# Weight parts in tiles of 1024 columns, one split for several products of a block of seven, and variances issued first

## The chip, the cores and the metric

The kernel runs on one core of one Trainium2 chip. The metric is the device time of one execution in microseconds (us). Three runs of the kernel before the change give a median of 1121.44 us (1121.39 to 1121.47).

## The reference

A two-layer transformer in float32 over 512 tokens of width 1024, with 256 memory tokens. Layer 0 mixes tokens by a gated chunk mixing (gMLP) and attends to the memory; layer 1 mixes by causal attention with forget gates ("fox") and attends to the memory. Each layer ends in a gated feed-forward of hidden width 2816.

```python
for layer in range(DEPTH):
    a = rmsnorm(h, ln_mix_pre[layer])
    mem_n = rmsnorm(mem, ln_mem[layer])
    ...   # main: spatial gating (layer 0) or forgetting attention (layer 1)
    mixed = jnp.concatenate([main, memory_attention(q_mem, mem_n, w_mem_kv[layer])], axis=-1)
    h = h + rmsnorm(mixed @ w_out[layer], ln_mix_post[layer])
    f = rmsnorm(h, ln_ffn_pre[layer])
    f = (jax.nn.silu(f @ w_ffn_gate[layer]) * (f @ w_ffn_up[layer])) @ w_ffn_down[layer]
    h = h + rmsnorm(f, ln_ffn_post[layer])
```

## The kernel before, in words

**Split products.** TensorE (PE) multiplies fp32r numbers. To keep the accuracy, each operand is split in two parts: `split` (L240-241) casts the value to fp32r on ScalarE (ACT), which is `whi`, and VectorE (DVE) subtracts that from the value, which is `wlo`. `mm3` (L191-195) then issues three matmuls per product: high by high (L193), high weights by low inputs (L194), low weights by high inputs (L195). So the first two of three need only `whi`, the third needs `wlo`.

**Weights.** SyncE (SP) loads 128x1024 fp32 values (512 KB) into one of four `raw` tiles. Their parts go to rings of eight tiles of 128x512 for `whi` and eight for `wlo` (`pair_of_parts`). A part is used by the PE until its tile comes free for a later part; a cast that finds no free tile waits for the PE, and everything behind it on ACT waits too, since each engine takes its instructions in the order in which they were issued.

**Blocks of seven.** Gate and up weights of the feed-forward are multiplied by Strassen's scheme in Winograd's form (class `Seven`): 8 half-width products become seven of 12 matmuls of 128x256, 84 in all, for 1024x256 weights. A block loads two raw tiles, w1 = (a11, a12) and w2 = (a21, a22). `sums` (L966) forms on DVE s3 = a11+a21 (L970), then rewrites the raw values in place: a21 (L972), a11 (L974), a12 (L975). Product 1 takes a11 before and product 2 a12 before they are rewritten; products 6 and 3 take a11 and a12 after, 5 and 4 take a21 and a22, 7 takes s3. Outputs are the PSUM tiles `a` (products 1, 6, 5), `e` (7, 4) and `x` (2, 3). ACT copies an output out after products 1 (L988), 5 (L997), 6 (L1000) and 7 (L1003); `end` (L1005) adds on DVE: L1008 (e), L1009 (a), L1011 (x), and then the rows of the gate or up side (L1063-1071). Two blocks, one for gate and one for up, make a pair. The order of products in a block is 1, 7, 2, 6, 4, 3, 5; in the first pair of each layer, whose inputs are ready one after the other, it is 1, 2, 3 of both blocks, then 7 and 6 of both, then 4 and 5 of both (`sevens`, L1017). Each layer has 10 pairs in four groups, with the down products of a group (L1117-1126) between.

**Norms.** `Norm.finish` (L281) has the PE sum squares into `st`, DVE adds epsilon (`var`, L292), GpSimd (POOL) raises to the power -1/2 (`r`, L262), and the PE broadcasts the result by transposes (`rb`, L259). The memory's norm in layer 0, and two halves at each boundary before a feed-forward or before layer 1's queries, go this way.

**What sets the order.** A scheduler of the tile framework places each instruction on its engine by its own estimate of when it is ready and by program order as priority; the source does not fix it. In layer 0's last pair, the normed memory of layer 1 (`mparts`, 8 activations and 8 DVE operations) is made between the last two blocks.

## Time and profile before

| | |
|---|---|
| median of 3 runs | 1121.44 us |
| profiled execution | 1121.42 us |
| its span, granted PE clock | 1119.7 us, 0.999 |
| PE busy | 1107.3 us (99%) |
| DVE busy | 892.0 us (80%) |
| ACT busy | 660.3 us (59%) |
| POOL busy | 28.5 us (3%) |
| HBM read | 104.71 MB |
| casts `whi` <- raw, 128x512 | 460, 276.2 us, mean 620 ns |
| subtractions `wlo`, 128x512 | 460, 305.2 us, mean 685 ns |

The span runs from the first to the last recorded instruction; 1.7 us of the profiled time lie outside it. Rows of the timeline give the start and the duration in us, the engine, the source line, the operation, output and inputs by name, the shape and the number of instructions of a run, and in brackets how long the engine was idle before and what released it. Matmuls overlap: a 128x256 matmul is recorded with 0.28 us, and the next starts 0.12 us after it.

The program's places in the trace of before: layer 0's mixing from 0 to 165 us, the boundary to 210, its feed-forward to 527, layer 1's queries to 595, fox attention to 760, a boundary to 798, layer 1's feed-forward from there.

### The profile page before, as it was taken

What the parts mean: (1) busy time and instruction counts of PE and PEld (TensorE: products, weight loads), DVE (VectorE), ACT (ScalarE), POOL (GpSimd) and SP (SyncE); (2) the same over time, 40 slices, a digit from 0 to 9 for tenths busy, and PEclk for the clock granted to TensorE, in tenths of its full rate; (3) what the DMA queues carried; (4) which work ended last, traced back from release to release, by engine and by line L of the source; (5) the groups of instructions that cost most, each with busy time, mean ns of one, the idle gap of its engine ahead of it and who ended that gap; (6) DMA issues with size and microseconds to landing.
All of it is one profiled execution on the core that took longest, in us unless ns stands there. A gap on an engine that the chain in (4) does not pass through costs nothing.

```text
span 1119.7 us, 19536 instructions
## 1 busy us (share of the span) xinstructions
PE 1107.3 (99%) x7409; PEld 1002.7 (90%) x7409; DVE 892.0 (80%) x1721; ACT 660.3 (59%) x1388; POOL 28.5 (3%) x41
## 2 busy tenths in 40 slices
PE   8999999999999999999999999999999999999998
PEld 6998889999899899998988898889999899899996
DVE  7979448999598578796968889958998598588776
ACT  7775458755266255476757677768765266255453
POOL 0100001000000000001000000001000000000000
PEclk9999999999999999999999999999999999999999
DMA  7413231334224234244242655421235234233222
GB/s 265 151 49 109 77 97 58 100 108 151 76 89 140 74 99 127 76 135 148 63 128 59 153 128 137 135 76 57 65 106 152 74 101 133 70 109 118 76 76 76
DMA packets 63557, 118.12 MB, mean 105 GB/s; under 512 B 5164, under 2 KB 39992, under 8 KB 63464
## 3 DMA queue, kind: packets, MB, share of 16 engines
q1 hardware_dynamic: 62584, 116.05, 33.8%
q8 instruction: 58, 0.95, 0.4%
q0 software_dynamic: 192, 0.52, 0.2%
q10 hardware_dynamic: 688, 0.31, 0.1%
q14 instruction: 35, 0.29, 0.1%
HBM read 104.71 MB, written 2.10 MB: 95 GB/s over the span
## 4 chain that ended last, share of the span: by engine, by line
PE 86%; DVE 7%; ACT 3%; issue 2%; POOL 1%; DMA 1%; SPq 0%; POOLq 0%; DVEq 0%; ACTq 0%
PE y L193 9%; PE y L195 9%; PE y L194 9%; PE a L194 5%; PE a L193 5%; PE a L195 5%; PE ps L195 3%; PE ps L194 3%; PE ps L193 3%; PE e L193 3%; PE e L194 3%; PE x L194 3%; PE x L193 3%; PE x L195 3%; PE e L195 3%; DVE wlo L241 2%
## 5 line engine op out<-in xcount | busy, mean ns | idle before, releaser
L241 ACT CAST whi<-raw 128x512 fp32r<-128x512 f32 x460 | 276.2, 620 | 267.0 <-PE y L195 118.6
L241 DVE TENSOR_TENSOR wlo<-raw,whi 128x512 fp32r<-128x512 f32 x460 | 305.2, 685 | 108.8 <-ACT whi L241 106.6
L193 PE MATMUL y<-whi,fhi 128*128 128x512 f32 (+1 forms) x356 | 140.0, 394 | 0.0
L194 PE MATMUL y<-wlo,fhi 128*128 128x512 f32 (+1 forms) x356 | 139.4, 392 | 0.0
L195 PE MATMUL y<-whi,flo 128*128 128x512 f32 (+1 forms) x356 | 139.4, 392 | 0.0
L194 PE MATMUL a<-xslo,whi 128*128 128x256 f32 x320 | 90.0, 281 | 0.0
L194 PE MATMUL x<-xslo,whi 128*128 128x256 f32 x320 | 89.9, 281 | 0.0
L195 PE MATMUL x<-xshi,wlo 128*128 128x256 f32 x320 | 89.9, 281 | 0.0
L193 PE MATMUL x<-xshi,whi 128*128 128x256 f32 x320 | 89.8, 281 | 0.0
L193 PE MATMUL a<-xshi,whi 128*128 128x256 f32 x320 | 89.8, 281 | 0.0
L195 PE MATMUL a<-xshi,wlo 128*128 128x256 f32 x320 | 89.8, 281 | 0.0
L193 PEld LDWEIGHTS y<-whi,fhi 128*128 128x128 f32 x356 | 66.9, 188 | 15.7 <-ACT fhi L241 0.7
L195 PEld LDWEIGHTS y<-whi,flo 128*128 128x128 f32 x356 | 66.9, 188 | 15.5 <-DVE flo L241 0.2
L194 PEld LDWEIGHTS y<-wlo,fhi 128*128 128x128 f32 x356 | 67.0, 188 | 14.7 <-DVE wlo L241 0.2
L193 PE MATMUL ps<-xshi,whi 128*128 128x256 f32 (+1 forms) x224 | 67.5, 304 | 0.0
L195 PE MATMUL ps<-xshi,wlo 128*128 128x256 f32 (+1 forms) x224 | 67.1, 302 | 0.1
L194 PE MATMUL ps<-xslo,whi 128*128 128x256 f32 (+1 forms) x224 | 66.4, 299 | 0.0
L193 PEld LDWEIGHTS a<-xshi,whi 128*128 128x128 f32 x320 | 60.4, 189 | 0.4
L194 PEld LDWEIGHTS a<-xslo,whi 128*128 128x128 f32 x320 | 60.3, 188 | 0.3
L193 PEld LDWEIGHTS x<-xshi,whi 128*128 128x128 f32 x320 | 60.4, 189 | 0.0
L195 PEld LDWEIGHTS x<-xshi,wlo 128*128 128x128 f32 x320 | 60.3, 189 | 0.0
L194 PEld LDWEIGHTS x<-xslo,whi 128*128 128x128 f32 x320 | 60.3, 188 | 0.0
(283 smaller groups left out, 3091.1 us busy)
## 6 DMA issues: line engine op xcount, KB each, us to landing
raw<-in_w_gate SPq DMA_DIRECT2D x44, 512.0 KB, 3.6
raw<-in_w_up SPq DMA_DIRECT2D x44, 512.0 KB, 3.5
raw<-in_w_down SPq DMA_DIRECT2D x44, 512.0 KB, 4.0
raw<-in_w_out SPq DMA_DIRECT2D x16, 512.0 KB, 4.5
raw<-in_w_b_q SPq DMA_DIRECT2D x8, 512.0 KB, 3.5
raw<-in_w_a_v SPq DMA_DIRECT2D x6, 512.0 KB, 7.0
raw<-in_w_a_u SPq DMA_DIRECT2D x6, 512.0 KB
raw<-in_w_v SPq DMA_DIRECT2D x6, 512.0 KB, 3.7
```

The source lines that it names most:

```text
L193: PE.matmul(o, w[0], x[0], start=start, stop=False, skip_group_check=more)
L194: PE.matmul(o, w[0], x[1], start=False, stop=False, skip_group_check=more)
L195: return PE.matmul(o, w[1], x[0], start=False, stop=stop, skip_group_check=more)
L241: last_parts[:] = A.copy(hi, src), (eng or V).tensor_sub(lo, src, hi)
```

## The change

It does three things.

1. The rings of parts hold four tiles of 128x1024 in place of eight of 128x512, of the same bytes. `prepared` weights still are split in steps of 512 columns, but into the two halves of one tile, which comes free when the whole tile has been used.
2. Where 1024 columns are split for products that lie close together, one cast and one subtraction do it: in a block of seven for products 1 and 2, for 6 and 3, for 5 and 4 (product 7 stays alone with 512 columns, in a tile of 1024), in the down products between groups, and in the gate weights `w_a_u` of layer 0. On ACT and on DVE each, 316 instructions of 512 columns become 158: 126 of 128x1024 and 32 of 128x4x2x128. DVE goes from 1721 to 1563 instructions.
3. `var` and `rsqrt` of `Norm.finish` are issued with high priority.

PE, POOL and SP have the same number of instructions as before; what the scheduler does with the new sizes moves some of them. `var` of the memory's norm in layer 0 stands right behind the first `q` product on DVE, ahead of 5 `mparts` and 8 subtractions, where it had 4 of these subtractions and the `mparts` before it, and its `rb` stands 12 matmuls earlier on the PE. At the boundaries the first half's `var` and its `rb` stand earlier too, `rb` by 11 matmuls. The order is the same in both layers at the first two of the following places.

**Place 1: ACT, first pair of a feed-forward (layer 0).** `raw_2506` holds w1 of the first block, `raw_2569` w1 of the second; `a_2511` is the output of product 1 of the first block. Before:

```order
L1095 COPY y_2436<-y_2486 128x512
L1095 COPY y_2437<-y_2494 128x512
L241 CAST whi_2553<-raw_2506 128x512
L988 COPY s_1_2513<-a_2511 128x256
L241 CAST whi_2580<-raw_2569 128x512
```

Now, with `raw_2432` and `raw_2491` for the two w1, `a_2437` for that output, `whi_2475` for products 6 and 3 of the first block and `whi_2502` for 1 and 2 of the second:

```order
L1108 COPY y_2362<-y_2412 128x512
L1108 COPY y_2363<-y_2420 128x512
L1001 COPY s_1_2439<-a_2437 128x256
L246 CAST whi_2475<-raw_2432 128x1024
L246 CAST whi_2502<-raw_2491 128x1024
L246 CAST whi_2534<-raw_2491 128x1024
L1001 COPY s_2_2498<-a_2496 128x256
```

The cast for product 3 stood ahead of the copy of product 1's output and now stands behind it, with twice the columns. On the PE the rows that follow product 2 (`whi_2443` in tile 1) now are:

```order
L200 MATMUL x_2436<-xshi_1960,wlo_2444 128x256
L198 MATMUL x_2436<-xshi_2103,whi_2475 128x256
L199 MATMUL x_2436<-xslo_2104,whi_2475 128x256
L198 MATMUL a_2437<-d2hi_2327,whi_2475 128x256
L199 MATMUL a_2437<-d2lo_2328,whi_2475 128x256
L198 MATMUL a_2496<-xshi_1874,whi_2502 128x256
L199 MATMUL a_2496<-xslo_1875,whi_2502 128x256
L198 MATMUL x_2495<-xshi_1923,whi_2502 128x256
L200 MATMUL x_2436<-xshi_2103,wlo_2476 128x256
```

Where the 12 matmuls of product 3 followed in a piece, two of product 3, two of product 6, two of product 1 of the second block and one of its product 2 now come before the first that reads a low part.

**Place 2: ACT, the third block (first of the second pair).** Before, `whi_2850` (product 6), `whi_2867` (4), `whi_2883` (3) and `whi_2899` (5) are the parts of the third block:

```order
L241 CAST whi_2850<-raw_2786 128x512
L241 CAST whi_2867<-raw_2788 128x512
L241 CAST whi_2883<-raw_2786 128x512
L997 COPY s_1_2513<-a_2511 128x256
L241 CAST whi_2899<-raw_2788 128x512
L1064 ACTIVATE s_1_2514<-s_1_2514 128x512
L997 COPY s_2_2576<-a_2574 128x256
L1064 ACTIVATE s_1_2513<-s_1_2513 128x512
L241 CAST whi_2934<-raw_2923 128x512
L988 COPY s_3_2793<-a_2791 128x256
```

Now these are `whi_2748` (6 and 3) and `whi_2765` (5 and 4):

```order
L1010 COPY s_1_2439<-a_2437 128x256
L1077 ACTIVATE s_1_2440<-s_1_2440 128x512
L1010 COPY s_2_2498<-a_2496 128x256
L1077 ACTIVATE s_1_2439<-s_1_2439 128x512
L1001 COPY s_3_2695<-a_2693 128x256
L246 CAST fhi_2430<-s_2_2499 128x512
L1016 COPY s_3_2696<-e_2694 128x256
L246 CAST fhi_2428<-s_2_2498 128x512
L246 CAST whi_2748<-raw_2688 128x1024
L246 CAST whi_2765<-raw_2690 128x1024
```

The casts stood ahead of the closing of the first pair (the activations L1064) and now stand behind it, and behind the copies of the third block's own products 1 (`a_2693`) and 7 (`e_2694`, L1016). On the PE, product 7 is followed by the 12 matmuls of product 2, then two of 6, two of 3 and two of 4, and then those that read low parts.

**Place 3: DVE, the last block of layer 0 (the twentieth).** Before, `wlo_5823` is for product 7, `wlo_5852` for 6:

```order
L246 SCALAR_TENSOR_TENSOR mparts_5643<-mem_5617,gains,mparts_5643 128x256
L1008 TENSOR_TENSOR s_19_5658<-e_5656,s_19_5658 128x256
L975 TENSOR_TENSOR raw_5787<-raw_5787 128x512
L241 TENSOR_TENSOR wlo_5823<-s_20_5796,whi_5822 128x512
L241 TENSOR_TENSOR wlo_5852<-raw_5787,whi_5851 128x512
```

Now `wlo_5453` is for product 7, `wlo_5482` for 6 and 3:

```order
L251 SCALAR_TENSOR_TENSOR mparts_5289<-mem_5263,gains,mparts_5289 128x256
L1021 TENSOR_TENSOR s_19_5304<-e_5302,s_19_5304 128x256
L1022 TENSOR_TENSOR s_19_5304<-a_5301,s_19_5304 128x256
L1024 TENSOR_TENSOR s_19_5303<-x_5300,s_19_5303 128x512
L1076 TENSOR_TENSOR s_19_5304<-s_19_5304,rbc 128x512
L1076 TENSOR_TENSOR s_19_5303<-s_19_5303,rbc 128x512
L983 TENSOR_TENSOR raw_5421<-raw_5421 128x512
L246 TENSOR_TENSOR wlo_5453<-s_20_5430,whi_5452 128x512
L246 TENSOR_TENSOR wlo_5482<-raw_5421,whi_5481 128x1024
```

Four more operations of the nineteenth block's end (L1022, L1024, twice L1076) stand between the eight `mparts` and the low part of product 7.

The diff; left out are the edits that only carry the new argument on, and the query weights of layer 0, the value weights of layer 1 and the fox heads' parts, which now take the halves of one tile:

```diff
--- before.py
+++ after.py
@@ -130,11 +130,12 @@
     A.activation(early, avg, AF.Copy, scale=2.0)
 
 
-    def pair_of_parts(n=512, aside=False):
-        if aside:
-            return act("whi"), act("wlo")
-        return (wp.tile([P, max(n, 512)], F32R, tag="hi", name=name("whi"), bufs=8)[:, :n],
-                wp.tile([P, max(n, 512)], F32R, tag="lo", name=name("wlo"), bufs=8)[:, :n])
+    def pair_of_parts(n=1024):
+
+        return [wp.tile([P, max(n, 1024)], F32R, tag=t, name=name(f"w{t}"), bufs=4)[:, :n] for t in ("hi", "lo")]
+
+    def columns(pair, c0, c1):
+        return [t[:, c0:c1] for t in pair]
 
     def cut(pair, w):
 
@@ -146,32 +147,36 @@
         last_load[0] = nc.sync.dma_start(raw, src)
         return raw
 
-    def prepared(src, shape, eng=None):
+    def prepared(src, shape, step=512):
 
         raw = wp.tile([P, 1024], F32, tag="raw", name=name("raw"), bufs=4)
         n = shape[0] * shape[1]
         dst = raw[:, :n].rearrange("p (a b) -> p a b", a=src.shape[1]) if len(src.shape) == 3 else raw[:, :n]
         last_load[0] = nc.sync.dma_start(dst, src)
-        return weight_parts(raw, shape, eng)
-
-    def weight_parts(raw, shape, eng=None):
+        return weight_parts(raw, shape, step)
+
+    def weight_parts(raw, shape, step=512):
         n = shape[0] * shape[1]
-        parts = []
-        for d in range(0, n, 512):
-            pair = pair_of_parts(min(512, n - d))
-            split(raw[:, d : min(d + 512, n)], *pair, eng)
-            parts += cut(pair, shape[1])
-        return parts
-
-    def moving_pair(src, aside=False):
+        pair = pair_of_parts(n)
+        for c in range(0, n, step):
+            at = c, min(c + step, n)
+            split(raw[:, at[0] : at[1]], *columns(pair, *at))
+        return cut(pair, shape[1])
+
+    def moving_pair(src, aside=False, whole=False):
 
         raw = wp.tile([P, 1024], F32, tag="raw", name=name("raw"), bufs=4)
         last_load[0] = nc.sync.dma_start(raw.rearrange("p (m c) -> p m c", m=4), src)
         four = raw.rearrange("p (m k c) -> p m k c", m=4, k=2)
+        pair = [] if aside else pair_of_parts()
+        if whole:
+            split(four, *(t.rearrange("p (k m c) -> p m k c", m=4, k=2) for t in pair))
         parts = []
         for x in range(2):
-            hi, lo = (t.rearrange("p (m c) -> p m c", m=4) for t in pair_of_parts(aside=aside))
-            split(four[:, :, x, :], hi, lo)
+            both = (act("whi"), act("wlo")) if aside else columns(pair, 512 * x, 512 * x + 512)
+            hi, lo = (t.rearrange("p (m c) -> p m c", m=4) for t in both)
+            if not whole:
+                split(four[:, :, x, :], hi, lo)
             parts.append((hi, lo))
         return parts
 
@@ -289,8 +294,9 @@
                 for n, sq in enumerate(some):
                     PE.matmul(st[:, tb : tb + 1], sq, avg, start=n == 0, stop=n == len(some) - 1)
             v = small("var")
-            V.tensor_scalar_add(v[:, t0:t1], st[:, t0:t1], RMS_EPS)
-            rsqrt(self.r4[:, t0:t1], v[:, t0:t1], t1 - t0)
+            with tc.high_priority():
+                V.tensor_scalar_add(v[:, t0:t1], st[:, t0:t1], RMS_EPS)
+                rsqrt(self.r4[:, t0:t1], v[:, t0:t1], t1 - t0)
 
         def sums(self, tb, cols):
             return [self.acc[:, c + tb * P : c + (tb + 1) * P] for c in range(0, T, self.width)]
...
@@ -679,7 +685,7 @@
 
             def gate_inputs(m):
                 while len(wu) < min(m + 2, NG):
-                    wu.append(prepared(i["w_a_u"][len(wu)], (KT, P)))
+                    wu.append(prepared(i["w_a_u"][len(wu)], (KT, P), 1024))
                 [o] = group([wu[m]], a, FULL, ["mm"])
                 us.append(plain("u"))
                 V.tensor_mul(us[m], o, rbc)
@@ -952,54 +958,61 @@
 
         def __init__(self, xs, src, tag, rows):
             self.xs, self.rows = xs, rows
-            w1, w2 = loaded(src(0)), loaded(src(1))
-            self.a = [w[:, d : d + 512] for w in (w1, w2) for d in (0, 512)]
+            self.raws = loaded(src(0)), loaded(src(1))
+            self.a = [w[:, d : d + 512] for w in self.raws for d in (0, 512)]
             self.x, self.p = ps(tag, s="x"), ps(tag, (P, 256), s="a")
             self.q = ps(tag, (P, 256), s="e")
             self.s1, self.s2 = prob("s1"), prob("s2")
-
-        def parts(self, src):
-            pair = pair_of_parts()
+            self.w = {}
+
+        def parts(self, src, *which):
+            n = 512 * len(which)
+            pair = pair_of_parts(n)
             split(src, *pair)
-            return pair
+            for x, n in enumerate(which):
+                self.w[n] = columns(pair, 512 * x, 512 * x + 512)
 
         def sums(self):
 
             a11, a12, a21, a22 = self.a
             self.s3 = temp("s3")
             V.tensor_add(self.s3, a11, a21)
-            self.w1 = self.parts(a11)
+            self.parts(self.raws[0], 1, 2)
             V.tensor_add(a21, a21, a22)
-            self.w2 = self.parts(a12)
             V.tensor_add(a11, a21, a11)
             V.tensor_add(a12, a11, a12)
 
         def product(self, o, w, n, more=False):
-            for k, w in enumerate(cut(w, P)):
+            for k, w in enumerate(cut(self.w[w], P)):
                 mm3(o, w, self.xs[n][k], k == 0 and not more, k == KT // 2 - 1, more)
 
         def run(self, what):
 
-            a11, a12, a21, a22 = self.a
             left, right = (slice(*c) for c in HALVES)
             s1, s2 = self.s1, self.s2
+            if what in (3, 6) and 3 not in self.w:
+                self.parts(self.raws[0], 6, 3)
+            elif what in (4, 5) and 4 not in self.w:
+                self.parts(self.raws[1], 5, 4)
+            elif what == 7:
+                self.parts(self.s3, 7)
             if what == 1:
-                self.product(self.p, self.w1, 0)
+                self.product(self.p, 1, 0)
                 A.copy(s1[:, left], self.p)
             elif what == 2:
-                self.product(self.x[:, left], self.w2, 2)
+                self.product(self.x[:, left], 2, 2)
             elif what == 3:
-                self.product(self.x[:, right], self.parts(a12), 5)
+                self.product(self.x[:, right], 3, 5)
             elif what == 4:
-                self.product(self.q, self.parts(a22), 4, True)
+                self.product(self.q, 4, 4, True)
             elif what == 5:
-                self.product(self.p, self.parts(a21), 6, True)
+                self.product(self.p, 5, 6, True)
                 A.copy(s1[:, right], self.p)
             elif what == 6:
-                self.product(self.p, self.parts(a11), 3, True)
+                self.product(self.p, 6, 3, True)
                 A.copy(s2[:, left], self.p)
             else:
-                self.product(self.q, self.parts(self.s3), 1)
+                self.product(self.q, 7, 1)
                 A.copy(s2[:, right], self.q)
 
         def end(self):
@@ -1117,7 +1130,7 @@
             for dh in range(2):
                 outs = [ps("mm" if tb < 2 else "lg", s="y") for tb in range(TB)]
                 for kp in range(nk // 2):
-                    w = down_weights(layer, k0 + 2 * kp, dh)
+                    w = down_weights(layer, k0 + 2 * kp, dh, whole=True)
                     for x in range(2):
                         k = 2 * kp + x
                         for tb in range(TB):
...
```

20 lines of the change are left out of this document (10 added, 10 removed).

## The prediction

> **What bounds the kernel now.** I read the page first, then windows, then the timeline at the places where the order of instructions changes.
>
> ```profile
> PE 1107.3 (99%) x7409; PEld 1002.7 (90%) x7409; DVE 892.0 (80%) x1721; ACT 660.3 (59%) x1388; POOL 28.5 (3%) x41
> ...
> PE 86%; DVE 7%; ACT 3%; issue 2%; POOL 1%; DMA 1%; SPq 0%; POOLq 0%; DVEq 0%; ACTq 0%
> ...
> L241 ACT CAST whi<-raw 128x512 fp32r<-128x512 f32 x460 | 276.2, 620 | 267.0 <-PE y L195 118.6
> L241 DVE TENSOR_TENSOR wlo<-raw,whi 128x512 fp32r<-128x512 f32 x460 | 305.2, 685 | 108.8 <-ACT whi L241 106.6
> ```
>
> PE is busy 99% of the span and carries 86% of the chain, so time saved on DVE or ACT counts only where PE waits for them. Of ACT's 267 us of idle time before the casts, 118.6 end with one group of matmuls (y, L195) that frees a tile: the parts are normally made far ahead. The window of the first three pairs of blocks of seven shows the other side: DVE is nearly full there.
>
> ```profile
> 205.00:266.00 61.00, 61.00 (x492) 59.61 (x491) 57.90 (x103) 38.85 (x81) 0.00 (x0) 1.00 0.34 109
> ```
>
> In this stretch (PE 61.00, PEld 59.61, DVE 57.90, ACT 38.85 us of 61) PE never pauses, though DVE has only 3 us to spare. So this change can win the few waits of PE, and it can make new ones where a part comes later than now. Base of the sum is the profiled execution, 1121.42 us (span 1119.7), 0.02 below the median.
>
> **Prices.** No row has 1024 columns. The nearest have 256:
>
> ```profile
> L241 DVE TENSOR_TENSOR vals<-vf,vals 128x256 fp32r<-128x256 f32 x12 | 4.9, 418 | 0.4 <-ACT vals L241 0.3
> ...
> L241 ACT CAST vals<-vf 128x256 fp32r<-128x256 f32 x12 | 4.8, 404 | 1.3 <-DVE vf L1217 1.3
> ```
>
> ACT: 620 - 404 = 216 ns per 256 columns, so 1024 take 620 + 432 = 1.05 us. DVE: 685 - 418 = 267, so 685 + 534 = 1.22 us. Back to back the records overlap: three casts in 1.67 us (228.37, below) are 0.53 apart, four subtractions in 2.50 (41.31, below) 0.605. So what follows a 1024 cast starts 0.53 + 0.43 = 0.96 after it, and 0.605 + 0.53 = 1.14 after a 1024 subtraction. Bounds: above, two of 512 in a row (1.15 and 1.29 us long); below, 256 columns at half this slope (0.84 and 0.95). I take the straight line, since both ends of it are measured. Each of 158 merges then saves 0.1 us of ACT and 0.07 of DVE, 16 and 11 us in all. On PE's path that is nothing: PE covers it by working 61 of 61 us. But whoever needs the first half of a merged part gets it 0.43 (ACT) or 0.53 (DVE) later.
>
> [...]
>
> **What the change can win.** In the trace PE stops at four places that it touches.
>
> ```profile
> 34.49 2.89 POOL L262 TENSOR_TENSOR r<-var,mhalf 128x2 f32<-128x2 f32 x1 [7.56 <-DVE var L292]
> 35.44 0.28 PE L195 MATMUL ps<-mparts,wlo 128*128 128x256 f32 x1
> 37.44 0.43 PE L259 MATMUL rb<-ident,r 128*128 128x128 f32 x2 [1.73 <-POOL r L262]
> 37.91 0.42 DVE L305 COPY rmem<-rb 128x256 f32<-128x256 f32 x1 [1.09 <-PE rb L259]
> 41.31 2.50 DVE L241 TENSOR_TENSOR wlo<-raw,whi 128x512 fp32r<-128x512 f32 x4
> ...
> 184.72 0.50 PE L290 MATMUL st<-avg,sq 128*128 128x1 f32 x4
> 186.86 0.15 DVE L292 TENSOR_SCALAR var<-st 128x2 f32<-128x2 f32 x1
> 187.76 0.28 PE L194 MATMUL ps<-xslo,whi 128*128 128x256 f32 x1
> 188.22 0.43 PE L259 MATMUL rb<-ident,r 128*128 128x128 f32 x2 [0.18 <-POOL r L262]
> ...
> 265.74 0.28 PE L195 MATMUL a<-d2hi,wlo 128*128 128x256 f32 x1
> 266.44 0.39 PE L193 MATMUL e<-t,whi 128*128 128x256 f32 x1 [0.42 <-ACT s L1003]
> ...
> 775.73 0.28 PE L194 MATMUL ps<-xslo,whi 128*128 128x256 f32 x1
> 776.17 0.43 PE L259 MATMUL rb<-ident,r 128*128 128x128 f32 x2 [0.16 <-POOL r L262]
> ```
>
> A matmul normally starts 0.12 after the one before. So the boundaries cost 0.46 - 0.12 = 0.34 (188.22) and 0.44 - 0.12 = 0.32 (776.17); the end of the third pair 0.70 - 0.12 = 0.58 (266.44), where DVE, full since the first pair, has fallen behind; the memory's norm 2.00 - 0.12 = 1.88. At the boundaries `st` ends at 184.72 + 0.50 = 185.22, but `var` came at 186.86, behind DVE operations that it now passes: up to 1.6 us earlier, while `rb` is asked for 11 x 0.118 = 1.3 earlier. What is left, 0.3, is about the wait: 0.66 won (bounds 0 and 0.66). At 266 DVE will have 18 merges times 0.07 = 1.3 us less before it, more than the wait: 0.58 won. At the memory's norm `var` goes ahead, but DVE's work up to the memory's values stays the same: it loses the 1.09 idle before `rmem`, and gets a new pause at `var`, which now waits for `st`.
>
> ```profile
> 28.68 1.28 DVE L646 SCALAR_TENSOR_TENSOR q<-ps,rbc 128x512 f32<-128x512 f32 x2
> 29.02 0.95 PE L290 MATMUL st<-avg,acc 128*128 128x1 f32 x8
> ```
>
> `st` ends at 29.97, the first `q` at 28.68 + 0.61 = 29.29: 0.7 idle and 0.1 for `var`. The 5 `mparts`, 8 subtractions and `rmem` behind it come about 0.3 earlier, and so do the low parts of the memory's value weights (41.31), which PE needs next. PE will wait there in place of here: 0.30 won of 1.88 (bounds 0 and 1.88). Together 0.66 + 0.58 + 0.30 = 1.54.
>
> **Place 1, the first pair, costs 0.63 in each layer.**
>
> ```profile
> 211.40 0.62 ACT L241 CAST whi<-raw 128x512 fp32r<-128x512 f32 x1 [0.15 <-DVE raw L975]
> 211.78 0.28 PE L195 MATMUL a<-xshi,wlo 128*128 128x256 f32 x1
> 212.05 0.69 DVE L241 TENSOR_TENSOR wlo<-raw,whi 128x512 fp32r<-128x512 f32 x1
> 212.10 0.37 ACT L988 COPY s<-a 128x256 f32<-128x256 f32 x1
> 212.37 1.15 ACT L241 CAST whi<-raw 128x512 fp32r<-128x512 f32 x2
> 213.33 0.28 PE L193 MATMUL x<-xshi,whi 128*128 128x256 f32 x1
> ```
>
> The cast for product 3 began at 211.40 and PE used it at 213.33. Now the copy stands ahead; it comes 0.32 after the last matmul of product 1 (211.78, 212.10), and the cast can begin at 212.37. It ends at 213.42, and with 0.05 for the signal (211.40 + 0.62 to 212.05: 0.03) PE may go on at 213.47: 0.14 late. The next cast, for products 1 and 2 of the second block, begins 0.96 later at 213.33, ends at 214.38, is seen at 214.43. PE wants it after the four matmuls that the scheduler put between, at 213.47 + 4 x 0.118 = 213.94: 0.49 late. The low parts follow at 213.47 + 1.22 = 214.69 and 1.14 later, and PE asks for them at 214.79 and 216.0: no wait. So 0.14 + 0.49 = 0.63, and the same in layer 1, whose order is the same.
>
> **Place 2, the third block, costs 1.39 in each layer.**
>
> ```profile
> 228.37 1.67 ACT L241 CAST whi<-raw 128x512 fp32r<-128x512 f32 x3 [1.15 <-DVE raw L974]
> ...
> 233.11 0.28 PE L195 MATMUL e<-t3hi,wlo 128*128 128x256 f32 x1
> 234.67 0.28 PE L193 MATMUL a<-d2hi,whi 128*128 128x256 f32 x1
> 235.12 0.38 ACT L1003 COPY s<-e 128x256 f32<-128x256 f32 x1
> 235.38 0.64 ACT L241 CAST fhi<-s 128x512 fp32r<-128x512 f32 x1
> ```
>
> Before, the parts for product 6 are made from 228.37, six us before PE needs them at 234.67. Now their cast is behind the copy of product 7, which cannot start before the matmul at 233.11 is through. Counted from that matmul: copy at 0.32, `fhi` 0.26 later (235.12 to 235.38), the cast 0.53 after that, at 1.11; ready and seen at 1.11 + 1.05 + 0.05 = 2.21. PE is there at 234.67 - 233.11 = 1.56: 0.65 late. The next cast, for 5 and 4, is ready 0.96 later, at 3.17; PE asks after four matmuls, at 2.21 + 0.47 = 2.68: 0.49 late. Then it asks for the low part of 6, at 3.17 + 0.24 = 3.41. DVE can start that at 2.16 at best, done at 3.43; but four operations of 0.605 (L983, `flo`, s3, `flo`) stand ahead, behind the closing of the first pair. I put 0.25, between 0 and 0.8. Sum 0.65 + 0.49 + 0.25 = 1.39.
>
> **Place 3, the last block of layer 0, costs 0.94.**
>
> ```profile
> 480.68 0.42 DVE L1009 TENSOR_TENSOR s<-a,s 128x256 f32<-128x256 f32 x1
> 482.02 0.28 PE L195 MATMUL e<-t3hi,wlo 128*128 128x256 f32 x1
> 485.25 3.25 DVE L246 SCALAR_TENSOR_TENSOR mparts<-mem,gains,mparts 128x256 fp32r<-128x256 f32 x8
> 488.42 0.41 DVE L1008 TENSOR_TENSOR s<-e,s 128x256 f32<-128x256 f32 x1
> 488.76 0.68 DVE L975 TENSOR_TENSOR raw<-raw 128x512 f32<-128x512 f32 x1
> 490.69 0.28 PE L193 MATMUL e<-t3hi,whi 128*128 128x256 f32 x1
> ```
>
> The tile for products 1 and 2 of the twentieth block now comes free with product 7 of the nineteenth (482.02). Cast about 482.25 to 483.30, subtraction from 483.35, the next at 484.49; `flo`, L982 and `flo` take three times 0.605 to 486.30; the eight `mparts` 3.17 (485.25 to 488.42) to 489.47. Then L1021 and L1022 (0.33 each), L1024, twice L1076 and L983 (four times 0.605) to 492.55, and the low part of product 7 until 493.23, seen at 493.28. PE begins that product at 490.69, goes through two matmuls of it and twelve of product 2, and asks at 490.69 + 14 x 0.118 = 492.34: 0.94 late. What comes next has caught up by then. Layer 1's last pair has no `mparts`.
>
> **Sum.** 2 x (0.63 + 1.39) + 0.94 = 4.98 lost, 1.54 won: 1121.42 + 3.44 = **1124.9 us, slower by 0.3%**. By the bounds of the prices the losses lie between 3.0 and 6.1 and the gains between 1.0 and 2.9: 1121.5 to 1126.5 at the extremes, 1123.2 to 1126.4 as this forecast's own range.
>
> **Rivals.** *DVE was the brake and larger operations release it; faster.* For it: 57.90 of 61 us, and the wait at 266.44. Then the parts stay ahead at all three places and every wait above goes: 0.66 + 0.58 + 1.88 = 3.12, 1118.3 us. Against it: PE has no pause in that window, and place 2 hangs on ACT's order, not on DVE's load. It decides if the casts at places 1 and 2 begin more than 1.2 us earlier than I put them. [...]
> *Places 2 and 3 are hidden.* If the closings run earlier than I think and the casts keep a lead, only place 1 stays: 1121.42 - 1.54 + 1.26 = 1121.1. Against: the copy of product 7 is ahead of the cast whatever DVE does.
> *Merged operations cost as much as two.* Casts of 1.15 and subtractions of 1.29 make place 1 0.82, place 2 1.7 and place 3 1.05, 6.1 in all; DVE stays full and the wait at 266.44 remains, so 0.96 is won: 1126.5. The rows of 256 speak against it.
> *The priority does not do what it says*: POOL's `r` took 2.89 us at 34.49, against 0.98 here, and could land as late as now. Then only 0.58 is won: 1121.42 + 4.98 - 0.58 = 1125.8.
>
> ```profile
> 187.18 0.98 POOL L262 TENSOR_TENSOR r<-var,mhalf 128x2 f32<-128x2 f32 x1 [11.82 <-DVE var L292]
> ```
>
> **Chances.** Forecast 0.45, DVE released 0.11, places 2 and 3 hidden 0.24, no saving by merging 0.13, priority without effect 0.07. What a measurement of this kernel can tell from no change is 0.2%, 2.2 us: faster is below 1119.2, slower above 1123.7. Faster 0.11; the second rival (0.24) and a tenth of the forecast (0.04) lie within, 0.28; the rest is slower, 0.61. The range, 1120.8 to 1126.8, leaves out the first rival and the upper end.
>
> **What would show it.** In the new trace: PE idle at place 1 ended by ACT `whi` (0.1 to 0.2, then 0.4 to 0.6); at place 2, in both layers, three pauses of PE ended by `whi`, `whi` and `wlo`; in layer 0's last pair one of about 0.9 ended by DVE `wlo`; no wait at 266 and none for `rb`, but one at the memory's values. Casts of 1024 columns at 1.05 us, subtractions at 1.22. The forecast is wrong if these casts begin before the copies that stand ahead of them let them, or if PE's pauses move elsewhere.

## The result and the profile after

The changed kernel takes 1127.01 us (median of six runs, 1126.26 to 1129.70) against 1121.45 (1121.20 to 1121.63): a ratio of 1.0052, 95% interval 1.0040 to 1.0065. It is slower by 0.5%, 5.6 us where 3.5 were forecast. Its profiled execution takes 1127.39 us (span 1125.7), 5.97 more than that of before. From its page, the busy time of each engine and then the chain of work that ended last:

```profile
PE 1109.5 (99%) x7408; PEld 1002.9 (89%) x7409; DVE 883.0 (78%) x1561; ACT 638.2 (57%) x1228; POOL 24.8 (2%) x41
...
PE 86%; DVE 7%; ACT 3%; issue 2%; DMA 1%; POOL 0%; SPq 0%; POOLq 0%; DVEq 0%; ACTq 0%
```

ACT lost 22 us of work and DVE 9, and none of it reached the end. (DVE has 1561 instructions, two fewer than said above: the small weights `wf` of the fox stage are now split in two pieces of 48 columns in place of four of 24.) The merged operations, from the groups by shape (busy us, mean ns, idle before):

```profile
L246 ACT CAST whi<-raw 128x1024 fp32r<-128x1024 f32 x158 | 164.9, 1050 | 227.8 <-PE y L200 95.9 <-PE x L199 51.4 <-PE e L199 33.6
L246 DVE TENSOR_TENSOR wlo<-raw,whi 128x1024 fp32r<-128x1024 f32 x158 | 191.7, 1223 | 88.6 <-ACT whi L246 88.6
```

What PE waited for (total us, times, longest), and the matmuls behind these waits from the timeline of PE, with the idle time before them in brackets:

```profile
PE e L200 <- DVE wlo L246: 3.3, 3, 1.5
PE a L198 <- ACT whi L246: 2.0, 4, 1.0
...
PE memv L199 <- DVE wlo L246: 1.2, 1, 1.2
...
PE rb L264 <- POOL r L267: 0.5, 1, 0.5
```

```profile
40.91 0.39 PE L199 MATMUL memv<-wlo,mparts 128*128 128x256 f32 x1 [1.24 <-DVE wlo L246]
...
212.95 0.38 PE L198 MATMUL a<-xshi,whi 128*128 128x256 f32 x1 [0.21 <-ACT whi L246]
...
234.70 0.39 PE L198 MATMUL a<-d2hi,whi 128*128 128x256 f32 x1 [0.57 <-ACT whi L246]
235.65 0.39 PE L198 MATMUL e<-t,whi 128*128 128x256 f32 x1 [0.20 <-ACT whi L246]
248.85 0.39 PE L200 MATMUL e<-t,wlo 128*128 128x256 f32 x1 [1.51 <-DVE wlo L246]
...
494.25 0.39 PE L200 MATMUL e<-t3hi,wlo 128*128 128x256 f32 x1 [1.31 <-DVE wlo L246]
...
815.22 0.39 PE L200 MATMUL e<-t,wlo 128*128 128x256 f32 x1 [0.49 <-DVE wlo L246]
...
826.13 0.39 PE L198 MATMUL a<-d2hi,whi 128*128 128x256 f32 x1 [1.00 <-ACT whi L246]
827.07 0.38 PE L198 MATMUL e<-t,whi 128*128 128x256 f32 x1 [0.21 <-ACT whi L246]
827.89 0.40 PE L200 MATMUL a<-d2hi,wlo 128*128 128x256 f32 x1 [0.32 <-DVE wlo L246]
```

The one `rb` wait left (0.5) is that of the first norm, which was there before; those at both boundaries and the one at 266 us are gone. The waits at places 1, 2 and 3 have come, and two more, at 248.85 and 815.22. Between the same matmuls (the two traces laid beside each other by the number of the matmul), the time went:

| stretch (us of before) | before | after | difference |
|---|---|---|---|
| start, 0 to 24 | 22.81 | 22.13 | -0.68 |
| memory's norm and values, 24 to 60 | 36.10 | 35.70 | -0.40 |
| mixing and boundary, 60 to 208 | 147.99 | 147.63 | -0.36 |
| first pair, to 222 (place 1) | 13.95 | 14.79 | +0.84 |
| third block, to 236 (place 2) | 13.99 | 15.56 | +1.57 |
| fourth block on, to 262 | 26.00 | 27.58 | +1.58 |
| to 480 | 217.95 | 215.96 | -1.99 |
| last pair, to 500 (place 3) | 20.02 | 21.61 | +1.59 |
| queries, fox, boundary, to 797 | 297.09 | 295.87 | -1.22 |
| layer 1: first pair to 812 (place 1) | 14.95 | 15.90 | +0.95 |
| layer 1: to 833 (place 2) | 20.94 | 25.47 | +4.53 |
| rest | 282.45 | 282.03 | -0.42 |

Two rows cannot be read as waits. From 275 to 480 us PE waits for nothing in either trace and yet needs 1.4 us less. And behind place 2 in layer 1 the clock falls; the stretches of the changed kernel (us; PE, PEld, DVE, ACT, POOL busy, with instructions; granted clock; DMA share, GB/s):

```profile
824.00:828.00 4.00, 2.48 (x17) 1.87 (x16) 4.00 (x7) 4.00 (x7) 0.00 (x0) 1.00 0.01 4
828.00:831.50 3.50, 3.50 (x18) 3.50 (x19) 2.70 (x3) 0.86 (x2) 0.00 (x0) 0.52 0.72 202
```

In this stretch matmuls start 0.21 us apart (16 steps from 828.11 to 831.50), where 0.118 is usual: 1.5 us lost.

### The profile page after: what moved, and what is told of

Read it like the earlier page. It is cut to its first block, busy times and chain, and to the rows that moved or that the text cites. A ratio compares the mean times of both kernels' runs of the same rounds, so it can differ in the third digit from the quotient of the medians.

```text
span 1125.7 us, 19058 instructions
## 1 busy us (share of the span) xinstructions
PE 1109.5 (99%) x7408; PEld 1002.9 (89%) x7409; DVE 883.0 (78%) x1561; ACT 638.2 (57%) x1228; POOL 24.8 (2%) x41
## 4 chain that ended last, share of the span: by engine, by line
PE 86%; DVE 7%; ACT 3%; issue 2%; DMA 1%; POOL 0%; SPq 0%; POOLq 0%; DVEq 0%; ACTq 0%
PE y L198 9%; PE y L200 9%; PE y L199 9%; PE a L200 4%; PE a L199 4%; PE a L198 4%; PE ps L200 4%; PE ps L198 4%; PE ps L199 4%; PE e L200 3%; PE e L198 3%; PE e L199 3%; PE x L200 3%; PE x L199 3%; PE x L198 3%; DVE wlo L246 3%
## 5 line engine op out<-in xcount | busy, mean ns | idle before, releaser
L246 ACT CAST whi<-raw 128x1024 fp32r<-128x1024 f32 (+1 forms) x302 | 247.7, 844 | 260.9 <-PE y L200 97.4
L246 DVE TENSOR_TENSOR wlo<-raw,whi 128x1024 fp32r<-128x1024 f32 (+1 forms) x302 | 285.4, 967 | 98.3 <-ACT whi L246 98.0
L200 PEld LDWEIGHTS a<-xshi,wlo 128*128 128x128 f32 x320 | 60.4, 189 | 0.0
```

Of the source, the lines that this page charges most:

```text
L200: return PE.matmul(o, w[1], x[0], start=False, stop=stop, skip_group_check=more)
L246: last_parts[:] = A.copy(hi, src), (eng or V).tensor_sub(lo, src, hi)
```

## The experiments

The experiments ran on different chips, so each ratio is to runs of the kernel before on the same chip, and I compare these ratios. Each has an interval of about 0.13% to either side, so a difference of two of them is uncertain by some 2 us. E1 means the run whose label begins with e1, and so on.

**Which of the three parts does it (E1 to E4)?** My theory was that the merging makes the casts late, behind the closings of the pair before. The rival was that the coarser ring does it.

E1 takes the priority from the changed kernel:

```diff
-            with tc.high_priority():
-                V.tensor_scalar_add(v[:, t0:t1], st[:, t0:t1], RMS_EPS)
-                rsqrt(self.r4[:, t0:t1], v[:, t0:t1], t1 - t0)
+            V.tensor_scalar_add(v[:, t0:t1], st[:, t0:t1], RMS_EPS)
+            rsqrt(self.r4[:, t0:t1], v[:, t0:t1], t1 - t0)
```

> The changed kernel with the third part undone: var and rsqrt of the norms at ordinary priority; coarse rings and merged splits stay. If the priority wins what its places in the two traces show (the two rb waits of 0.34 and 0.32, and 1.89 - 1.40 = 0.49 at the memory's norm), this kernel is 1.1 us slower than the changed one: 1128.2, with PE waiting for POOL r near 187 and 776 us again. Rival, that the priority had no effect or took something elsewhere: 1127.0 or less.

E2 is the same lines the other way round, in the kernel before.

> The kernel before with the third part alone: var and rsqrt at high priority, tiles of 512 and single splits as they were. By the same sum 1121.4 - 1.1 = 1120.3, and no new wait in the two feed-forwards. Rival, that the gain needs the lighter DVE of the merged kernel: 1121.4, with the waits at the memory's norm and at 266 us as before.

Measured: E1 1126.86, ratio 1.0051 (1.0038 to 1.0063), the same as with priority. E2 1121.08, ratio 0.9998 (0.9989 to 1.0007): no change. The 1.1 us in question are 0.1%, no more than these intervals, so the times alone cannot exclude them; the traces show where they go. E1's has the `rb` waits again (2.4 us in three), as expected, and the loss is made up later. In E1 PE comes 1.1 us later to the fourth block, and its wait at 248 us shrinks from 1.68 to 0.35, since it hangs on a load that lands at 242.8 to 243.0 in both. DVE in the changed kernel (L979 is the addition s3 of the fifth block):

```profile
240.54 0.68 DVE L983 TENSOR_TENSOR raw<-raw 128x512 f32<-128x512 f32 x1
242.96 0.69 DVE L979 TENSOR_TENSOR s<-raw,raw 128x512 f32<-128x512 f32 x1 [1.74 <-DMA raw<-in_w_gate]
...
246.37 1.28 DVE L1076 TENSOR_TENSOR s<-s,rbc 128x512 f32<-128x512 f32 x2
247.57 2.36 DVE L246 TENSOR_TENSOR wlo<-raw,whi 128x1024 fp32r<-128x1024 f32 x2
```

And in E1:

```profile
242.82 0.69 DVE L978 TENSOR_TENSOR s<-raw,raw 128x512 f32<-128x512 f32 x1 [0.42 <-DMA raw<-in_w_gate]
```

E2 gives its gain back at another load: PE waits at 860 us, at the down products, for a closing (L1010) that stands on DVE behind low parts of weights that came late.

```profile
PE y L193 <- DVE s L1010: 1.4, 1, 1.4
PE memv L194 <- DVE wlo L241: 1.3, 1, 1.3
```

E3 keeps the rings of 1024 but lets each product of a block split its own 512 columns, where it did before:

```diff
-            if what in (3, 6) and 3 not in self.w:
-                self.parts(self.raws[0], 6, 3)
-            elif what in (4, 5) and 4 not in self.w:
-                self.parts(self.raws[1], 5, 4)
+            a11, a12, a21, a22 = self.a
+            if what in (3, 6):
+                self.half((a12, a11)[what == 6], what, (6, 3), what == 3)
+            elif what in (4, 5):
+                self.half((a21, a22)[what == 4], what, (5, 4), what == 4)
```

(`half` splits into one half of the shared tile; products 1 and 2 likewise.)

> The changed kernel in which the blocks of seven split each product's 512 columns by themselves and at the same place in the program as before, but into the halves of tiles of 1024: the coarse ring stays, the merging in the blocks goes (it stays in the down products and the gate weights). If the merging ties the casts to the last of their inputs and so loses at places 1 to 3, the waits there go: about 1120 to 1121. Rival, that the coarser ring (a tile comes free only when both halves are used) delays the casts: waits for whi and wlo stay at places 2 and 3, 1124 or more.

Measured: 1116.18, ratio 0.9954 (0.9942 to 0.9967). The coarse ring is not the loss; the kernel is faster than before, by more than I expected. No wait is left at places 1 and 2; two of 0.5 and 0.4 us stand at 244 and 486.

E4 puts the rewriting of the raw values first:

```diff
+            with tc.high_priority():
-            V.tensor_add(a21, a21, a22)
-            V.tensor_add(a11, a21, a11)
-            V.tensor_add(a12, a11, a12)
+                V.tensor_add(a21, a21, a22)
+                V.tensor_add(a11, a21, a11)
+                V.tensor_add(a12, a11, a12)
```

> The changed kernel with high priority for the three additions that rewrite the raw values in place (a21, a11, a12). The cast for products 6 and 3 reads both a11 and a12; in the third block the rewriting of a12 stood behind the ten closing operations of the first pair on DVE. With it ahead of them the casts stand ahead of the closing and of the copies on ACT. If this is the cause at place 2, the three waits there (1.35 us in layer 0, 2.0 in layer 1) and the stretch at half clock behind the second (1.6 us) go: 1127.0 - 5.0 = 1122 to 1123.5 with something given back elsewhere. Rival, that the late copy of product 7 or the DVE load alone makes the casts late: waits at place 2 stay over 1 us, 1126 or more.

Measured: 1122.06, ratio 1.0008 (0.9998 to 1.0017): 4.9 us won. On DVE and ACT the third block's a12 (L984) is now rewritten before the closing (L1023 to L1085), and the casts follow at once:

```profile
227.61 0.68 DVE L984 TENSOR_TENSOR raw<-raw 128x512 f32<-128x512 f32 x1
228.21 0.42 DVE L1023 TENSOR_TENSOR s<-a,s 128x256 f32<-128x256 f32 x1
```

```profile
228.38 1.05 ACT L246 CAST whi<-raw 128x1024 fp32r<-128x1024 f32 x1 [1.10 <-DVE raw L984]
229.72 1.05 ACT L246 CAST whi<-raw 128x1024 fp32r<-128x1024 f32 x1 [0.29 <-PE a L199]
```

In the changed kernel they began five microseconds later, behind the copy of product 7 (L1016):

```profile
232.81 0.37 ACT L1016 COPY s<-e 128x256 f32<-128x256 f32 x1
233.08 0.63 ACT L246 CAST fhi<-s 128x512 fp32r<-128x512 f32 x1
233.60 2.94 ACT L246 CAST whi<-raw 128x1024 fp32r<-128x1024 f32 x3
```

All waits of place 2 are gone in both layers, and so is the stretch at half clock (mean granted clock 1.000, and 0.998 in the changed kernel; one wait of 0.25 us, for another low part, stands at 823). So the merged cast waits for the last of its inputs (at 228.38 it has waited 1.10 us for L984): product 6 needs a11 alone, but its cast had to wait for a12.

**Where the time comes from that no wait explains (E5 to E8).** E3 is 5 us faster than the kernel before, and yet PE's gaps of over 0.06 us (from start to start, beyond the usual step) sum to as much in its trace (25.6 and 25.2 us). The pace of PE itself differs. I took the starts of all 128x256 matmuls that follow each other without a wait, and the addresses of their two tiles in the built program, modulo 128 bytes. The activations lie at 96. The slots of the parts were 2144 bytes apart and lay at four places; now they are 4288 apart (a slot is as large as the ring's largest tile, 1072 columns) and lie at 96 and 32 in turn. E5 makes the slots 4352 bytes, 34 x 128:

```diff
-        return [wp.tile([P, max(n, 1024)], F32R, tag=t, name=name(f"w{t}"), bufs=4)[:, :n] for t in ("hi", "lo")]
+        return [wp.tile([P, max(n, 1088)], F32R, tag=t, name=name(f"w{t}"), bufs=4)[:, :n] for t in ("hi", "lo")]
```

E6 does the same and moves them by 64; E7 is this in E3, E8 in the kernel before (with 544 for 512):

```diff
+    shift = wp.tile([P, 16], F32, tag="shift", name=name("shift"), bufs=1)
+    V.memset(shift, 0.0)
     zero = zeros()
```

> The changed kernel, in the same order on every engine; only the slots of the two rings of parts are 4352 bytes apart in place of 4288. In the traces so far a 128x256 matmul of the changed kernel starts 119.1 ns after the one before where the addresses of its inputs' tile and of its weights' tile differ by a multiple of 128 bytes, and 116.4 ns where they differ by 64 more; half of the slots are of each kind. Here all are of the first kind. If the address decides, the mean of 4514 such matmuls goes from 117.8 to about 119.1 and the time to 1127.0 + 6 = 1133; if the two kinds only go together with something else (which product, which slot), 1127.0.

> The same with slots of 4352 bytes and the rings moved by 64 bytes (a tile of 16 columns ahead of them, written once): all weights' slots are of the second kind. If the address decides: mean 116.4 or less, 1127.0 - 6 = 1121, less what a faster PE waits more; if not, 1127.0.

> The kernel with the coarse ring but single splits in the blocks of seven (1116.2), with all weights' slots of the second kind. There the two kinds took 119.0 and 115.5 ns, 2288 and 2269 matmuls: 2288 x 3.5 = 8 us less, 1108 to 1110. If the address does not decide: 1116.2.

> The kernel before, slots of 2176 bytes in place of 2144 and the rings moved by 64 bytes. Its weights lie in four kinds now (differences of 0, 32, 64, 96 modulo 128: 118.6, 117.9, 117.5, 119.2 ns). If the address decides, all go to 115.5 to 117.5: 4568 x (118.3 - 116.5) = 8 us less, 1113; if not, 1121.4.

| kernel | time, us | ratio to before (95%) | ns per matmul, difference 0 | 32 | 64 | 96 | mean |
|---|---|---|---|---|---|---|---|
| before | 1121.45 | | 118.6 | 117.9 | 117.5 | 119.2 | 118.3 |
| changed | 1127.01 | 1.0052 (1.0040-1.0065) | 119.1 | | 116.5 | | 117.8 |
| E5, all at 0 | 1128.83 | 1.0064 (1.0052-1.0077) | 119.8 | | | | 119.8 |
| E6, at 64 | 1116.35 | 0.9953 (0.9939-0.9967) | 118.4 | | 114.7 | | 115.1 |
| E7, E3 at 64 | 1107.64 | 0.9875 (0.9861-0.9888) | 118.5 | | 114.5 | | 115.0 |
| E8, before at 64 | 1110.37 | 0.9901 (0.9887-0.9914) | 118.5 | | 115.1 | | 115.5 |

The addresses make the difference here. E5 has the changed kernel's order on every engine; E6 has one memset more and a few instructions in another place in its first 30 us. 12.5 us lie between them. The difference modulo 128 is not all of it: at 64 a matmul takes 117.5 ns in the kernel before, 116.5 in the changed one and 114.7 in E6. The expectations were right in direction and wrong in size. E5 was expected at 1133, but its matmuls of 512 columns became faster (230.9 to 227.9 ns, some 1780 of them: 5 us); E6, E7 and E8 came out below what was expected (1121, 1108 to 1110, 1113). The view by windows shows the pace as well: the same 40 us of layer 0's second group, blocks of seven alone and PE busy 40.00 in all, hold so many matmuls in before, changed, E5, E6 and E8:

```profile
312.00:352.00 40.00, 40.00 (x340) 40.00 (x339) 37.55 (x66) 25.66 (x53) 0.00 (x0) 1.00 0.34 106
```

```profile
312.00:352.00 40.00, 40.00 (x343) 40.00 (x342) 37.96 (x55) 24.16 (x41) 0.00 (x0) 1.00 0.35 106
```

```profile
312.00:352.00 40.00, 40.00 (x335) 40.00 (x335) 37.23 (x54) 23.64 (x41) 0.00 (x0) 1.00 0.35 103
```

```profile
312.00:352.00 40.00, 40.00 (x352) 40.00 (x352) 38.05 (x57) 23.81 (x40) 0.00 (x0) 1.00 0.33 107
```

```profile
312.00:352.00 40.00, 40.00 (x349) 40.00 (x349) 38.51 (x68) 26.35 (x54) 0.00 (x0) 1.00 0.33 105
```

With the addresses equal modulo 128, the change costs 6.0 us (E8 to E6) and its merging in the blocks 8.7 (E7 to E6, where the pace is the same, 115.0 and 115.1 ns). The rest of the change (ring, down and gate weights, priority) comes with 2.7 us less (E8 to E7); but there the pace still differs, 115.5 and 115.0 ns, which over some 4550 matmuls is 2.3 us, so no gain of the rest itself is shown.

**Which merge (E9 to E11)?** Each undoes one pair in E6, the other two stay. For E9 (E10 and E11 are alike, for products 1 and 2 and for 5 and 4):

```diff
-            if what in (3, 6) and 3 not in self.w:
-                self.parts(self.raws[0], 6, 3)
+            if what in (3, 6):
+                self.half(self.a[what == 3], what, (6, 3), what == 3)
```

> The changed kernel with all weights' slots on the faster side (1116.35), in which products 6 and 3 of a block split their 512 columns by themselves again, each at its product; 1 with 2 and 5 with 4 stay merged. If that pair is what holds the casts at places 1 and 2 back (its cast waits until a12 too is rewritten), the waits there go: 0.58 in each layer at place 1, 1.78 and 2.19 at place 2, and the 1.43 us at half clock behind the latter: 1116.35 - 6.5 = 1110. Rival, that any two merged splits do it: 1114 or more.

> The same with products 1 and 2 split singly, 6 with 3 and 5 with 4 merged. a12 can be rewritten only when the merged subtraction of 1 and 2 has read it. If that is the root at places 2 and 3, about 1116.35 - 4 = 1112; by the theory that the cast for 6 and 3 is the root, only place 3 (1.82 us) is touched: 1114.5.

> The same with products 5 and 4 split singly, the others merged. By the trace the waits for the low part of product 4 (1.77 us near 247, 0.84 near 809) hang on that pair: its merged subtraction comes behind an addition that waits for a load. They go: 1116.35 - 2.6 = 1113.7, places 1 and 2 stay. Rival, that they are only DVE's load: 1116.

Measured against E6's ratio of 0.9953: E9 1115.01 us, ratio 0.9935 (0.9922 to 0.9948); E10 1113.56, 0.9928 (0.9916 to 0.9940); E11 1117.25, 0.9962 (0.9950 to 0.9975). By the ratios that is -2.0, -2.8 and +1.0 us of the 8.7, and only the second is clear of the 2 us of uncertainty. All three expectations failed, and E9 and E11 came out as their rivals have it (1114 or more, 1116): no pair alone holds the loss. E9 has 0.2 and 0.3 us left at places 1 and 2 of layer 0, and a new wait of 2.4 at 243; E10 frees place 1 and moves place 2 of layer 0 one block on; in E11 product 4 no longer waits at 247, and PE waits at the down products, which E6 does not (E11's list of waits; the execution profiled, 1119.88 us, is the slowest of five):

```profile
PE y L200 <- DVE s L1030: 3.1, 4, 1.2
```

**The clock (E12).** Twenty matmuls of 128 columns fill PE's wait at place 2 of E6:

```diff
+            if what == 6 and self.number in (3, 23):
+                fill(20, self.last)
...
+    def fill(n, behind):
+        with tc.issue_after(behind.ins):
+            o = ps("tr", s="idle")
+            for _ in range(n):
+                PE.matmul(o[:, :P], ident_b, ident_b, start=True, stop=True)
```

> The changed kernel on the faster side (1116.35) with 20 more matmuls of 128 columns in the third block of each layer, ahead of product 6, where PE waits 0.94 and 1.35 us; their output is not used. If PE's idle time in the microseconds before is what halves the granted clock (0.52 from 823.1 to 826.3 us in the layer 1 of that kernel), that stretch does not come and the time is 1116.35 - 1.4 = 115.0 under 1116: 1114.9, with PE's waits there filled. Rival, that the clock falls for another reason: the stretch stays, 1116.4 to 1117.

(The 115.0 there is a slip of the pen; 1114.9 is meant.) Measured: 1113.71, ratio 0.9928 (0.9916 to 0.9940), all five runs within 0.8 us. E6, and then E12, at place 2 of layer 1:

```profile
819.00:823.00 4.00, 2.29 (x15) 1.69 (x15) 4.00 (x7) 4.00 (x7) 0.00 (x0) 1.00 0.01 4
823.00:826.50 3.50, 3.50 (x18) 3.50 (x19) 2.65 (x3) 0.81 (x2) 0.00 (x0) 0.52 0.70 204
```

```profile
818.00:822.00 4.00, 3.65 (x39) 3.20 (x39) 4.00 (x6) 3.56 (x5) 0.00 (x0) 1.00 0.01 2
822.00:825.50 3.50, 3.50 (x33) 3.50 (x32) 3.50 (x7) 0.37 (x1) 0.00 (x0) 1.00 0.84 290
```

Work that nobody needs made the kernel 2.8 us faster (by the ratios). By the traces 1.4 of it is the clock, which stays at 1.00; the waits at 809 and 247 us also became shorter, and why is open.

**The two missed or undersized waits (E13 to E15), and the fastest version (E16).** E13 issues the additions of a block behind the low part for products 5 and 4 of the block before (in E6); E14 makes `mparts` one pair earlier (in E6); E15 moves only the addition s3 of the fifth block; E16 is E7 with E14's edit.

```diff
-                with behind(ended if opens else ()):
+                with behind(ended if opens else last_parts[1:]):
                     u.sums()
```

```diff
-                if meanwhile and m == k1 - 2 and gi == len(groups) - 1:
+                if meanwhile and m == k1 - 4 and gi == len(groups) - 1:
```

```diff
-            V.tensor_add(self.s3, a11, a21)
+            with behind(last_parts[1:] if self.number == 5 else ()):
+                V.tensor_add(self.s3, a11, a21)
```

> The changed kernel on the faster side (1116.35), with the additions of each next block issued behind the subtraction for products 5 and 4 of the block before it. If the addition s3 that waits for its load is what makes that low part late, the wait of 1.77 us near 247 (and 0.84 near 809) goes, and 1116.35 - 1.8 to 2.6 = 1113.7 to 1114.5 is left if nothing else comes later for it; if DVE's load as a whole is the cause, the wait stays and the time is 1116 or more.

> The same kernel with the next layer's memory parts (mparts, 8 operations of 0.40 us on DVE) made one pair earlier, not between the last two blocks of layer 0. If they are what makes the low part of product 7 late there, the wait of 1.82 us near 488 goes: 1116.35 - 1.8 = 1114.5, provided the earlier pair has room for them. If the closing operations alone do it (five operations, 2.4 us), 0.5 us or less is won: 1116.

> The changed kernel on the faster side (1116.35); of layer 0's fifth block alone the addition s3, which waits for the block's load, is issued behind the low part for products 5 and 4 of the fourth block. If DVE's wait for that load is what makes the low part late, the wait of 1.77 us near 247 goes and DVE does not stand idle there; something of it comes back as a wait for the fifth block's product 7, whose part is made from s3: 1114.6 to 1116.35. If DVE's load as a whole is the cause, a wait of 1.5 us or more stays near 247.

> Single splits in the blocks of seven, all slots on the faster side (1107.64), and mparts one pair earlier. PE's waits near 481 and 487 us (0.42 and 0.25) go: 1107.0. If the earlier pair has no room, 1108 or more.

E13: 1203.24 us, ratio 1.0723 (1.0708 to 1.0737). The edit held back the splits of products 1 and 2 too, so it says nothing of 247. It shows the clock, though: PE stands 5.6 us at the first of twelve new waits, and then runs at half clock.

```profile
224.00:235.00 11.00, 5.44 (x47) 5.25 (x45) 7.86 (x15) 4.03 (x9) 0.00 (x0) 0.87 0.27 89
235.00:239.00 4.00, 3.94 (x18) 3.94 (x19) 2.99 (x5) 0.92 (x3) 0.00 (x0) 0.51 0.00 0
```

E14: 1113.70, ratio 0.9926 (0.9913 to 0.9938), 3.0 us less than E6. The wait of 1.8 at 488 is gone, and nothing came for it there: the `mparts` made place 3. That more than 1.8 is won fits the stretch at half clock in E6 (1.4 us), which E14's trace does not have (mean granted clock 0.999, and 0.998 in E6).

E15: 1120.73, ratio 0.9997 (0.9988 to 1.0006). The wait at 247 is gone: on DVE the low parts start at 245.51, two us earlier than in E6. But s3 is late now, and product 7 of the fifth block waits longer for its part than product 4 had, at half clock behind it (0.21 us from matmul to matmul, 257.89 to 260.87):

```profile
244.31 1.28 DVE L1081 TENSOR_TENSOR s<-s,rbc 128x512 f32<-128x512 f32 x2
245.51 2.35 DVE L248 TENSOR_TENSOR wlo<-raw,whi 128x1024 fp32r<-128x1024 f32 x2
...
254.99 1.28 DVE L984 TENSOR_TENSOR s<-raw,raw 128x512 f32<-128x512 f32 x2
```

```profile
256.38 0.39 PE L200 MATMUL e<-t3hi,whi 128*128 128x256 f32 x1 [4.04 <-ACT whi L248]
```

So the addition that stands on DVE and waits for its load caused the wait at 247, as the trace said; moving it only moves the wait.

E16: 1106.66, ratio 0.9868 (0.9855 to 0.9882), as expected (1107.0) and 1.3% faster than the kernel before. The intervals of E16 and E7 overlap, so that the times do not show the earlier `mparts` to win anything here.

## Why the prediction was right and wrong

The direction and the kind of the waits were right; the time, 1124.9, was 2.1 us too low and just outside the range. The step that failed is the sum of the losses. It ends with place 3 and has no term for product 4's low part (2.3 us measured) nor for the half clock behind a wait (1.5), and it takes the pace of the matmuls as fixed (3.4 us won). That it came so close is partly chance: large terms were missing on both sides. Waits are counted here from start to start, less the usual 0.12; the brackets above show less, since a matmul is recorded with 0.28.

- **Prices: right.** 1050 and 1223 ns against 1.05 and 1.22 us.
- **What the change can win (1.54): right in the trace, wrong as time.** Both `rb` waits and the one at 266 us went, and the memory's norm won 0.49 for 0.30. But the sum added the priority's terms as if PE kept them. Neither E1 nor E2 finds them in the time, and in E1's trace the next wait that hangs on a load is shorter by about as much (1.33) as PE comes later (1.1). By the prediction's own bounds, moreover, the gains lie between 0.58 and 3.12, not between 1.0 and 2.9, and its extremes are 1121.3 and 1126.9; the measured time lies outside these too.
- **Place 1 (0.63 in each layer): right.** 0.16 and 0.37 late in layer 0, 0.14 and 0.37 in layer 1.
- **Place 2 (1.39 in each layer): right in size in layer 0** (0.73, 0.37 and 0.26, sum 1.35), 2.00 in layer 1, and **wrong in the cause.** I held that "the copy of product 7 is ahead of the cast whatever DVE does". E4 shows that the order on ACT followed from DVE: with a12 rewritten early, the casts stand ahead of that copy.
- **Place 3 (0.94): undersized.** 1.47 and 0.17. The cause was right (E14); the chain on DVE began at 484.34 and not at 483.35, a first subtraction that I had put too early.
- **Missed: product 4's low part**, 1.68 near 248 and 0.64 near 815. The sum has no term for it; only the prediction's last sentence names the case, "if PE's pauses move elsewhere". It took the third block for the last place before place 3 where the order on DVE matters, and counted an addition s3 by its 0.605 us of work alone. The fifth block's s3 stood at 246.55 before, behind that low part:

```profile
245.34 1.28 DVE L241 TENSOR_TENSOR wlo<-raw,whi 128x512 fp32r<-128x512 f32 x2
246.55 0.68 DVE L970 TENSOR_TENSOR s<-raw,raw 128x512 f32<-128x512 f32 x1
```

The new order has it ahead, at 242.96, after DVE has stood 1.74 us for its load; moved behind, the wait at 247 goes (E15). Near 815, in layer 1's first pair, DVE stood 3.7 us before such an addition; this one was not tried, so its cause stays open.
- **Missed: what follows a wait.** Behind each wait some of the next matmuls start 0.1 us late; such gaps of 0.06 to 0.12 us sum up to 2.5 us more than before. And 1.5 us beyond the waits went at half clock; in E6 the granted clock behind the waits of place 2 was 0.52, and with these filled 1.00 (E12). Waits over 0.12 us in the two feed-forwards are 8.4 us, against 4.98 forecast.
- **Missed: the pace, about 3.4 us won.** 4568 matmuls by 0.45 ns and 1785 of 512 columns by 0.8 ns (231.7 to 230.9) are 3.5; the account of all gaps leaves 3.4. The prediction took 0.118 us for a property of the matmul. In E5 to E8 it goes with the tiles' addresses, from 114.5 to 119.8 ns, and the change moved these. Without this gain the kernel would have been slower by some 9 us (5.6 and 3.4, an estimate).
- Also unforeseen: 0.9 us fewer waits in the fox stage (595 to 760 us) and 0.7 at the start, where the query weights landed 0.67 earlier. Neither was tried; both may be of the run.
- **Rivals.** DVE's release did not come: E7 and E6 show that the large operations in the blocks cost 8.7 us here. E4 shows the mechanism for products 6 and 3, where two needs tied into one wait for the later input; for the other two pairs it is not shown singly. Places 2 and 3 were not hidden. A merged operation takes 1050 and 1223 ns, and not two casts' 1.15 or two subtractions' 1.29 us. The priority moved `var` and `r` ahead as it says, with nothing of it in the time.

## What to carry to other kernels

One operation for two uses waits for the later input and can serve the earlier need too late (4.9 us in E4); where PE never pauses, ask of each merge what its inputs wait for on the other engines, and not how much busy time it saves. A gain ahead of a wait that ends with a load can be given back there (1.1 us in E1), so add up gains only as far as the next such wait. When a pool's tile size changes, compare PE's pace in a stretch without waits (matmuls in 40 us), since the addresses have moved as well (12.5 us between E5 and E6).

## What the runs showed of the hardware

A 128x256 fp32r matmul with weights of 128x128 starts 114.5 to 115.1 ns after the one before where its two tiles' addresses differ by 64 modulo 128 bytes, and 118.4 to 119.8 where by 0 (E5 to E8). For 512 columns it is the other way round and smaller: 227.9 (E5) and 230.2 (E6). The difference counts, and not the place of the weights alone: in E6 the inputs of product 4 (tile `t4`) moved by 64 bytes as well, and their matmuls, on the same slots of weights, are most of those at difference 0, with 118.4. Why is open, and so is what sets the rest: the pace at 64 is 117.5 in the kernel before.

In the changed kernel and in E6 the granted clock fell to half for 3.41 us (828.13 to 831.54 and 822.97 to 826.39), after PE had been busy 2.5 and 2.3 of 4.0 us, with no single pause over 1.35 us. It did not fall each time: E14 has the same pauses as E6 at place 2 of layer 1 (1.34, 0.37, 0.47) and keeps the clock.

The traces show when. In that of the changed kernel the half clock lasts 3.413 us, and counted in periods of this length (822.61 us are 241 of 3.4133) the fall and the rise lie 241 and 242 behind the first rise of the clock, at 5.52, and the fall at the end, at 1125.09, 328. In the trace of before the only fall, at 1117.67, lies 326 behind the first rise, at 4.93; in E6 fall and rise lie 239 and 240 behind it. The period just ahead of the fall held 10 matmuls in E6 and 12 in the changed kernel (824.72 to 828.13; 10 of the 12 start in it, where 29 start in the period before). In E14 the end of a period so counted, at 819.71, lies between the first pause and the others, so that two periods share them, with 18 and 22 matmuls. The limit is not sharp in these counts: periods with 14 or 15 matmuls of 256 columns kept the clock in E6 (from 246.12 and 488.47) and E9 (241.69), and one with 15 lost it in E11 (489.44).

No pause at place 2 was as long as the 3.41 us of such a period (the longest was 1.35), and yet the clock fell behind one that was only partly idle; what sets it is not shown beyond these counts. The changed kernel's runs spread over 3.4 us and those of before over 0.4, which would fit none to two such stretches of 1.5 us lost each, an estimate (the two fastest of the six have a mean granted clock of 0.999, the others 0.998); only one of them was profiled.
